# Gate tiles at the ends of attention's halves and ahead of retention's last transposes, another order of the first loads, and other ends of stages, in a three-layer fp32 network on one core

## The chip, the core and the metric

The kernel runs on one NeuronCore of a Trainium2 chip. Times are device microseconds (us) of one execution. The engines are TensorE (PE: matrix products, its weight loads shown as PEld), VectorE (DVE), ScalarE (ACT), GpSimd (POOL, nearly unused here) and SyncE (SP), which issues the transfers (DMAs). Each engine works through its own instructions in order; engines wait for each other by semaphores.

## The reference, cut to what matters

The input is 512 tokens of width 1024, all in fp32. Two hybrid layers come first. Each has three branches that are gated and summed, then a product with a residual:

```
h = rms_norm(x, norm_g);  z = h @ w_in         # width 14848, split by branch
y_conv = conv_module(c_glu, c_gate, ...) @ w_conv_out      # 31 taps, LayerNorm, silu
y_ret  = retention_branch(r_q, r_k, r_v, r_gate, ...) @ w_ret_out      # 4 heads, both directions
y_attn = window_attention_branch(a_q, a_k, a_v, a_gate, ...) @ w_attn_out   # 16 heads, 4 kv heads
g = sigmoid(g_logit + b_gate)                  # one gate for each branch and column
x = x + (g[0] * y_conv + g[1] * y_ret + g[2] * y_attn) @ w_out
```

A third layer of another kind follows: a gated MLP over blocks of tokens, a gated linear recurrence with 8 heads (HGRN2), a LayerNorm after each residual, a small gated embedding (256 wide) and a feed-forward part 2816 wide with a last LayerNorm.

## The kernel before, in words

Activations lie in the on-chip memory (SBUF) with features on the partitions, as 8 tiles of 128 x 512, except where tokens are wanted on the partitions. All products are fp32 by three matmuls: each operand is split into a high part, cast to fp32r, and the remainder; `mm3` (lines 172 to 174) issues high x high, high x low and low x high into one accumulator. So a tile of 128 x 512 over 1024 inputs is 8 x 3 = 24 matmuls of 512 columns.

The weights come as 509 chunks of 512 KB in the order in which they are used. `_load_raw` (L128) issues a chunk's DMA on SP's queue; `_split_next` has ACT cast it (`hi`, L147 or L149) and DVE subtract (`lo`, L150). There are three buffers of each kind (WB = 3), so hi and lo are made up to two chunks ahead. `take` hands out blocks and splits further as it goes. Chunks in HOLD are kept in ordinary slots until several passes have used them.

The program is written as Python generators: one yields after each tile of a product ("dense" work), the other after each step of an attention or retention or recurrence core. `weave` alternates a step of the one with steps of the other. A scheduler then places every instruction on its engine by its own estimate of times, with the order in which the code issued them as priority. `issue_after` puts an instruction behind a named other one.

The seams that the change touches:

- the start: SP's queue sends the gains (`vkt`), the 8 tiles of x (L1414), the first weight chunks, then the constants (`ckt`, L1419) whose first 128 columns are the identity matrix. ACT and DVE scale and split x tile by tile; DVE also sums the squares (L210), and PE adds those up over partitions (L244). The matrix `two`, twice the identity, is made by DVE as soon as the constants come (L217).
- attention: `att_core(l, g)` does one half of the heads in 8 pieces: scores (L812), softmax on ACT and DVE, transposes (L789), products with v (L768, L769). `conv_ab` gives the dense tiles beside it. After the first half the second half's q is projected (`att_q`), normed and rotated on DVE while gate tiles run (`att_gate`), then transposed (L673); after the second half `branch_out` multiplies by w_attn_out, each output tile behind its own merge-gate tile.
- retention: for each of 4 heads `ret_core` does scores and values; at its end ACT copies the result (L607), DVE takes mean and variance, ACT normalizes (L223), and PE transposes (L624). `ret_gate` and `ret_qk` are the dense work.
- norms over tokens (`norm_tokens`, `norm_tile`): each tile of 128 tokens is normed on DVE with a reciprocal root made of small integer and float operations on one column (`rsqrt`), and transposed back (L363).
- HGRN2: `hg_core` steps of two heads alternate (`weave_gen`), and `weave2` runs them beside dense tiles; the scores are products at L1092.
- the last stage (`down`): tokens 256 to 511 (tiles 2 and 3) do the last weights one tile after the other, from weights kept in SBUF, then norm and store.

## Time and profile before

| what | value |
|---|---|
| median of 3 runs | 3061.37 us (3060.49 to 3064.32) |
| profiled execution, own time | 3065.6 us |
| its span in the trace | 3063.8 us |
| granted TensorE clock, mean | 0.996 |
| PE busy | 3009.6 us (98%), 13932 matmuls |
| DVE busy | 2089.7 us (68%) |
| ACT busy | 1161.2 us (38%) |
| DMA | 288.97 MB, mean 94 GB/s |

The span runs from the first instruction to the last. Busy time counts an engine's instructions; what is left is idle time, and the trace says what each idle stretch ended with. The granted clock is the share of full speed that TensorE was given: 1.00 stands for 2.4 GHz, 0.50 for 1.2 GHz. A matmul of 512 columns takes 0.39 us in the trace at full clock and overlaps the next one, and 0.63 us at half clock.

### The profile page before, as it was taken

What the parts mean: (1) busy time and instruction counts of PE and PEld (TensorE: products, weight loads), DVE (VectorE), ACT (ScalarE), POOL (GpSimd) and SP (SyncE); (2) the same over time, 40 slices, a digit from 0 to 9 for tenths busy, and PEclk for the clock granted to TensorE, in tenths of its full rate; (3) what the DMA queues carried; (4) which work ended last, traced back from release to release, by engine and by line L of the source; (5) the groups of instructions that cost most, each with busy time, mean ns of one, the idle gap of its engine ahead of it and who ended that gap; (6) DMA issues with size and microseconds to landing.
All of it is one profiled execution on the core that took longest, in us unless ns stands there. A gap on an engine that the chain in (4) does not pass through costs nothing.

```text
span 3063.8 us, 36027 instructions
## 1 busy us (share of the span) xinstructions
PE 3009.6 (98%) x13932; PEld 2455.5 (80%) x13932; DVE 2089.7 (68%) x3791; ACT 1161.2 (38%) x1867; POOL 0.2 (0%) x4
## 2 busy tenths in 40 slices
PE   8999999999999999999999999999999999999998
PEld 6777888887888877778888788887888888788887
DVE  7778897877444677989787754467776654743326
ACT  5546223334233455632333433333543333422222
POOL 0000000000000000000000000000000000000000
PEclk9999999999999999999999999999999999999999
DMA  4121222221223322122222132254222223422234
GB/s 156 63 76 56 90 90 76 79 76 67 96 96 127 121 69 69 57 89 97 72 73 76 65 101 96 96 180 143 84 89 70 69 76 121 161 93 99 98 110 151
DMA packets 83979, 288.97 MB, mean 94 GB/s; under 512 B 9440, under 2 KB 9696, under 8 KB 83680
## 3 DMA queue, kind: packets, MB, share of 16 engines
q1 hardware_dynamic: 83808, 286.68, 27.8%
q8 instruction: 109, 1.79, 0.2%
q14 instruction: 62, 0.51, 0.1%
HBM read 282.45 MB, written 4.19 MB: 94 GB/s over the span
## 4 chain that ended last, share of the span: by engine, by line
PE 87%; DVE 8%; ACT 3%; issue 1%; DMA 1%; SPq 0%; DVEq 0%; ACTq 0%
PE pm L172 20%; PE pm L173 20%; PE pm L174 20%; PE pa L172 7%; PE pa L174 7%; PE pa L173 7%; ACT s L223 2%; DVE s L213 2%; DVE lo L150 1%; DVE s L210 1%; PE pi L789 1%; DVE s L206 1%; PE pa L1092 1%; DVE pa L814 1%; ACT hi L149 1%
## 5 line engine op out<-in xcount | busy, mean ns | idle before, releaser
L172 PE MATMUL pm<-s,hi 128*128 128x512 f32 x2848 | 1117.8, 393 | 4.0 <-ACT s L205 1.5
L173 PE MATMUL pm<-s,hi 128*128 128x512 f32 x2848 | 1115.9, 392 | 1.3 <-DVE s L206 1.3
L174 PE MATMUL pm<-s,lo 128*128 128x512 f32 x2848 | 1112.8, 391 | 0.5 <-DVE lo L150 0.5
L149 ACT CAST hi<-raw 128x1024 fp32r<-128x1024 f32 x497 | 523.0, 1052 | 1375.8 <-PE pm L173 735.1
L150 DVE TENSOR_TENSOR lo<-raw,hi 128x1024 fp32r<-128x1024 f32 x500 | 610.2, 1220 | 484.7 <-ACT hi L149 478.4
L172 PEld LDWEIGHTS pm<-s,hi 128*128 128x128 f32 x2848 | 534.8, 188 | 120.4 <-ACT s L205 3.5
L174 PEld LDWEIGHTS pm<-s,lo 128*128 128x128 f32 x2848 | 535.1, 188 | 112.3 <-issue 2.2
L173 PEld LDWEIGHTS pm<-s,hi 128*128 128x128 f32 x2848 | 535.2, 188 | 112.0 <-DVE s L206 3.5
L213 DVE SCALAR_TENSOR_TENSOR s<-s,m,s 128x497 f32<-128x497 f32 (+10 forms) x528 | 390.3, 742 | 11.4
L172 PE MATMUL pa<-hi,s 128*128 128x512 f32 x830 | 331.7, 400 | 8.8 <-ACT hi L147 6.6
L173 PE MATMUL pa<-lo,s 128*128 128x512 f32 x830 | 329.5, 397 | 3.1 <-DVE lo L150 3.1
L174 PE MATMUL pa<-hi,s 128*128 128x512 f32 x830 | 328.9, 397 | 0.0
L213 DVE SCALAR_TENSOR_TENSOR s<-s,pm 128x512 f32<-128x512 f32 x164 | 111.9, 682 | 140.8 <-PE pm L174 140.2
L172 PEld LDWEIGHTS pa<-hi,s 128*128 128x128 f32 x830 | 158.3, 191 | 42.7 <-ACT hi L147 6.6
L173 PEld LDWEIGHTS pa<-lo,s 128*128 128x128 f32 x830 | 158.4, 191 | 36.9 <-DVE lo L150 5.4
L174 PEld LDWEIGHTS pa<-hi,s 128*128 128x128 f32 x830 | 158.4, 191 | 32.4
L205 ACT CAST s<-s 128x512 fp32r<-128x512 f32 x184 | 110.8, 621 | 177.9 <-DVE s L213 137.9
L206 DVE TENSOR_TENSOR s<-s,s 128x512 fp32r<-128x512 f32 x184 | 123.4, 688 | 29.6 <-ACT s L205 28.2
L210 DVE TENSOR_TENSOR s<-s,s 128x512 f32<-128x512 f32 (+2 forms) x178 | 114.2, 662 | 1.7
L223 ACT ACTIVATE s<-s 128x512 f32<-128x512 f32 (+1 forms) x130 | 79.2, 627 | 89.3 <-DVE s L217 24.7
L213 DVE SCALAR_TENSOR_TENSOR s<-s,s 128x512 f32<-128x512 f32 (+2 forms) x194 | 103.7, 554 | 7.8 <-ACT s L223 6.2
L223 ACT ACTIVATE s<-pa,m 128x256 f32<-128x256 f32 (+2 forms) x136 | 69.2, 524 | 53.0 <-DVE m L213 50.0
(161 smaller groups left out, 2350.8 us busy)
## 6 DMA issues: line engine op xcount, KB each, us to landing
raw<-w SPq DMA_DIRECT2D x509, 512.0 KB, 3.3
s<-xT SPq DMA_DIRECT2D x16, 256.0 KB, 5.1
xd<-s SPq DMA_DIRECT2D x8, 256.0 KB, 2.0
s<-xd SPq DMA_DIRECT2D x8, 256.0 KB, 5.6
out<-s SPq DMA_DIRECT2D x8, 256.0 KB, 3.7
s<-c_ln_g SPq DMA_DIRECT2D x6, 256.0 KB, 4.7
s<-c_ln_b SPq DMA_DIRECT2D x6, 256.0 KB, 5.2
ckt<-ck SPq DMA_DIRECT2D x1, 1344.0 KB, 6.2
```

Of the source, the lines that this page charges most:

```text
L149: self.A.copy(h, raw)
L150: self.V.tensor_tensor(out=l, in0=raw, in1=h.bitcast(F32), op=ALU.subtract)
L172: T.matmul(out, lhsT=lh, rhs=rh, start=start, stop=False)
L173: T.matmul(out, lhsT=lh, rhs=rl, start=False, stop=False)
L174: T.matmul(out, lhsT=ll, rhs=rh, start=False, stop=stop)
L205: self.A.copy(h, src)
L206: self.V.tensor_tensor(out=l, in0=src, in1=h.bitcast(F32), op=ALU.subtract)
L210: return self.V.tensor_tensor(out=out, in0=a, in1=b, op=op)
L213: return self.V.scalar_tensor_tensor(out=out, in0=a, scalar=s, in1=b, op0=op0, op1=op1)
L223: return self.A.activation(out, a, f, bias=bias, scale=scale, **kw)
L789: t = T.transpose(ps[:, i * 128:i * 128 + 128], pr[i][:, x * 128:x * 128 + 128], self.ck("ident"))
L814: self.V.tensor_tensor_reduce(out=sps[i][:, 0:w], in0=sps[i][:, 0:w], in1=mask, scale=1.0, scalar=-3.0e38, op0=ALU.add, op1=ALU.max, accum ...
```

## The change

It has seven parts.

1. First loads: the first weight chunk, then the first x tile, then the gains, then the rest as before. The doubling that makes `two` is issued after the weight transfer that `load_rest` waits for, instead of after the first loads.
2. Attention: two gate tiles of the second half (`att_gate(l, 1, 0..1)`) are appended to the dense work of the first half's core; two merge-gate tiles (`branch_gate(l, 2, 0)` and `(l, 2, 1)`) to that of the second half's core. `branch_gate` is the first part of `branch_out`, taken out; finished gates wait in `self.gates`, and `branch_out` takes them from there.
3. Retention: the last head's work is written out by hand. Two merge-gate tiles of retention's branch and the first step of its output product stand ahead of the core's last transposes, and the parts of earlier heads are split one by one as they are asked for.
4. Norms: `ahead` splits the next weight chunks before a late step; the second step of tile 2's transposes goes behind the last product, into the generator that the caller takes on.
5. `rsqrt` of one column: -0.5 v is made once, and each of the three rounds is two operations instead of three.
6. HGRN2: the first step of both heads of a pair is issued ahead of the pair's dense work.
7. Last stage: KEEP_2 = 2 more chunks are held, so that tiles 2 and 3 each do their last ten weights (30 matmuls) alone instead of six (18).

```diff
+HOLD = set(range(C_OUT, C_OUT + KEEP_0)) | set(range(C_O, C_O + KEEP_1)) | set(range(NCHUNK - WB - KEEP_2, NCHUNK - WB))
...
+    def ahead(self):
+        while self.nsplit <= min(self.pos // 8 + WB - 1, NCHUNK - 1):
+            self._split_next()
...
+        if self.pos >= 64:
+            self.ahead()
         yield ps
...
+        if n == 1:
+            w = self.small([128, 1])
+            self.ts(w, v, -0.5, None, ALU.mult)
         for _ in range(3):
-            self.tt(a, y, y, ALU.mult)
-            self.stt(a, a, -0.5, v, ALU.mult, ALU.mult)
+            if n == 1:
+                self.ts(a, y, y, w, ALU.mult, ALU.mult)
...
-                                ((3,), self.acc, {0: 2, 1: 1, 2: 1, 6: 2, 7: 2})):
+                                ((3,), self.acc, {0: 2, 1: 1, 2: 1, 7: 2})):
...
                 if k in at:
+                    self.ahead()
                     next(late[at[k]])
...
-        return late[3]
+        def left():
+            next(late[2])
+            for _ in range(3):
+                next(late[3])
+                yield
+        self.ahead()
+        return left()
...
+    def branch_gate(self, l, i, m):
+        pg = self.fm(("w_in", l), O_GL + i * D + m * 128, self.h)
+        t = self.slot()
+        self.act(t, pg, AF.Tanh, scale=0.5, bias=self.hbg[:, i * 8 + m:i * 8 + m + 1])
+        self.gates.append(t)
+        yield
...
         for m in range(KT):
-            pg = self.fm(("w_in", l), O_GL + i * D + m * 128, self.h)
...
+            if not self.gates:
+                yield from self.branch_gate(l, i, m)
+            t = self.gates.pop(0)
...
+        with self.tc.issue_after(self.ready.ins):
+            self.ts(self.two, self.ck("ident"), 2.0, None, ALU.mult)
...
-        self.weave(self.conv_ab(l, range(0, 4)), self.att_core(l, 0))
+        self.weave(chain(self.conv_ab(l, range(0, 4)), self.att_gate(l, 1, range(0, 2))), self.att_core(l, 0))
...
-        self.weave(self.att_gate(l, 1), qpost, 1)
-        self.weave(self.conv_ab(l, range(4, 8)), self.att_core(l, 1))
+        self.weave(self.att_gate(l, 1, range(2, 4)), qpost, 1)
+        self.weave(chain(self.conv_ab(l, range(4, 8)), self.branch_gate(l, 2, 0), self.branch_gate(l, 2, 1)), self.att_core(l, 1))
...
+        out = self.branch_out(l, 1, ("w_ret_out", l), ys)
+        core = self.ret_core(3)
+        for i, _ in enumerate(self.ret_gate(l, 3)):
+            self.unit()
+            if i == 3:
+                ys[2]
+            next(core)
         self.bg_rate = RATES[3]
...
+        self.go(self.branch_gate(l, 1, 0))
+        next(core)
+        next(core)
+        self.go(self.branch_gate(l, 1, 1))
+        next(out)
+        self.unit()
+        for _ in core:
+            pass
+        self.go(out)
...
             c = self.weave_gen(self.hg_core(2 * p), self.hg_core(2 * p + 1))
+            next(c)
+            next(c)
             self.weave2(dense(p), c)
...
-        for tiles, pool, kept in (((0, 1), self.mm, 0), ((2, 3), self.acc, 2 * WB)):
+        for tiles, pool, kept in (((0, 1), self.mm, 0), ((2, 3), self.acc, 2 * (WB + KEEP_2))):
...
-        nc.sync.dma_start(self.vkt[:, o:o + w], self.ap["vk"][:, o:o + w])
         xs = [self.slot() for _ in range(KT)]
+        self._load_raw()
         for k in range(KT):
             nc.sync.dma_start(xs[k], self.ap["xT"][k])
-            if k in (0, 2, 5):
+            if k == 0:
+                nc.sync.dma_start(self.vkt[:, o:o + w], self.ap["vk"][:, o:o + w])
+            if k in (2, 5):
                 self._load_raw()
```

How instructions move, at three places. Line numbers are those of each program: `mm3` is L172 to L174 before and L180 to L182 after, a scaling `stt` L213 and L223, a `tt` L210 and L220, the lo of a chunk L150 and L153, the doubling L217 and L227. Buffer numbers follow the underscore.

DVE at the program's start, before (`two` is the doubled identity, `lo` a chunk's remainder, s_125 the sum of squares):

```order
L213 SCALAR_TENSOR_TENSOR s_122<-s_93,vkt,s_121 128x512
L150 TENSOR_TENSOR lo_208<-raw_102,hi_207 128x1024
L213 SCALAR_TENSOR_TENSOR s_128<-s_94,vkt,s_127 128x512
L217 TENSOR_SCALAR two<-ckt 128x128
L210 TENSOR_TENSOR s_125<-s_125,s_131 128x512
L213 SCALAR_TENSOR_TENSOR s_135<-s_95,vkt,s_134 128x512
L150 TENSOR_TENSOR lo_214<-raw_106,hi_213 128x1024
L210 TENSOR_TENSOR s_125<-s_125,s_138 128x512
```

and after (the sum is s_124):

```order
L223 SCALAR_TENSOR_TENSOR s_121<-s_92,vkt,s_120 128x512
L153 TENSOR_TENSOR lo_207<-raw_100,hi_206 128x1024
L223 SCALAR_TENSOR_TENSOR s_127<-s_93,vkt,s_126 128x512
L220 TENSOR_TENSOR s_124<-s_124,s_130 128x512
L223 SCALAR_TENSOR_TENSOR s_134<-s_94,vkt,s_133 128x512
L153 TENSOR_TENSOR lo_213<-raw_106,hi_212 128x1024
L220 TENSOR_TENSOR s_124<-s_124,s_137 128x512
```

The doubling has left this place; the steps of the sum follow each other without it.

PE at the end of attention's first half in layer 0, before (L789: transposes of the probabilities, L768 and L769: products with v, then q's projection into pa_1786):

```order
L789 MATMUL pi_1678<-ckt,s_1610 128x128
L789 MATMUL pi_1678<-ckt,s_1609 128x128
L789 MATMUL pi_1678<-ckt,s_1607 128x128
L789 MATMUL pi_1678<-ckt,s_1608 128x128
L768 MATMUL pi_1728<-s_1674,s_369 128x512
L769 MATMUL pi_1728<-s_1675,s_369 128x512
L768 MATMUL pi_1728<-s_1683,s_372 128x512
L769 MATMUL pi_1728<-s_1684,s_372 128x512
L172 MATMUL pa_1786<-hi_1508,s_341 128x512
```

and after (the same transposes are L818; pm_1728 is a gate tile of the second half):

```order
L180 MATMUL pm_1728<-s_340,hi_1508 128x512
L181 MATMUL pm_1728<-s_341,hi_1508 128x512
L182 MATMUL pm_1728<-s_340,lo_1509 128x512
L818 MATMUL pi_1678<-ckt,s_1610 128x128
L818 MATMUL pi_1678<-ckt,s_1609 128x128
L818 MATMUL pi_1678<-ckt,s_1607 128x128
L818 MATMUL pi_1678<-ckt,s_1608 128x128
L180 MATMUL pm_1728<-s_345,hi_1508 128x512
L181 MATMUL pm_1728<-s_346,hi_1508 128x512
L182 MATMUL pm_1728<-s_345,lo_1509 128x512
L180 MATMUL pm_1728<-s_351,hi_1508 128x512
L181 MATMUL pm_1728<-s_352,hi_1508 128x512
```

A gate tile stands around the transposes, 24 matmuls of which three are ahead of them.

DVE at the program's end, before (s_21243 and s_21244 are tile 2's halves, s_21422 and s_21423 tile 3's; L1335 and L1339 are the statistics):

```order
L210 TENSOR_TENSOR s_21423<-s_21423,pa_23955 128x512
L210 TENSOR_TENSOR m_24178<-m_24177 128x1
L1335 BN_STATS m_23411<-s_21423 128x6
L213 SCALAR_TENSOR_TENSOR m_24178<-m_24178,m_24173 128x1
L1339 BN_AGGR m_24216<-m_23411 128x2
L213 SCALAR_TENSOR_TENSOR m_24177<-m_24178,m_24177 128x1
L217 TENSOR_SCALAR m_24217<-m_24216 128x1
L213 SCALAR_TENSOR_TENSOR s_21422<-s_21422,m_24216,s_23400 128x512
L213 SCALAR_TENSOR_TENSOR s_21243<-s_21243,m_24177,s_23404 128x512
L213 SCALAR_TENSOR_TENSOR s_21244<-s_21244,m_24177,s_23405 128x512
L217 TENSOR_SCALAR m_24220<-m_24217 128x1
L213 SCALAR_TENSOR_TENSOR s_21423<-s_21423,m_24216,s_23401 128x512
```

and after (tile 3's halves are s_21415 and s_21416, the statistics L1381 and L1385):

```order
L223 SCALAR_TENSOR_TENSOR m_24163<-m_24164,m_24163 128x1
L223 SCALAR_TENSOR_TENSOR s_21243<-s_21243,m_24163,s_23396 128x512
L223 SCALAR_TENSOR_TENSOR s_21244<-s_21244,m_24163,s_23397 128x512
L220 TENSOR_TENSOR s_21416<-s_21416,pa_23947 128x512
L1381 BN_STATS m_23403<-s_21416 128x6
L1385 BN_AGGR m_24213<-m_23403 128x2
L227 TENSOR_SCALAR m_24214<-m_24213 128x1
L223 SCALAR_TENSOR_TENSOR s_21415<-s_21415,m_24213,s_23392 128x512
L227 TENSOR_SCALAR m_24217<-m_24214 128x1
```

Before, tile 2's last steps stand between those of tile 3; after, they are ahead of tile 3's add.

## Rows read from the trace of the kernel before

**Rows 1.** the page: busy time of each engine, share of the span, instructions
```profile
PE 3009.6 (98%) x13932; PEld 2455.5 (80%) x13932; DVE 2089.7 (68%) x3791; ACT 1161.2 (38%) x1867; POOL 0.2 (0%) x4
```

**Rows 2.** waits of PE, whole span: us in total, times, longest us
```profile
PE pi L789 <- ACT s L223: 6.4, 18, 0.6
PE pa L1092 <- DVE s L210: 3.2, 4, 0.9
PE pa L173 <- DVE lo L150: 3.1, 4, 1.3
PE pi L363 <- DVE s L213: 2.5, 3, 1.9
...
PE pa L172 <- ACT s L223: 2.1, 2, 1.1
PE pi L789 <- DVE s L206: 2.0, 2, 1.0
PE pi L624 <- ACT s L223: 1.9, 6, 0.4
...
PE pm L172 <- ACT s L205: 1.5, 2, 0.8
PE pi L624 <- DVE s L213: 1.3, 2, 0.7
PE pm L173 <- DVE s L206: 1.3, 6, 0.2
...
PE pi L769 <- DVE s L206: 1.1, 2, 0.5
```

**Rows 3.** busy time by stretch: length, each engine, PEclk, DMA share, GB/s
```profile
26.00:32.80 6.80, 6.80 (x21) 5.64 (x21) 4.04 (x17) 0.00 (x0) 0.00 (x0) 0.50 0.32 111
169.40:172.70 3.30, 3.30 (x10) 2.52 (x9) 2.20 (x8) 1.72 (x5) 0.00 (x0) 0.50 0.00 0
303.00:309.00 6.00, 4.47 (x15) 2.28 (x14) 4.09 (x9) 3.60 (x7) 0.00 (x0) 1.00 0.22 81
2074.10:2077.40 3.30, 3.30 (x9) 2.13 (x8) 1.34 (x6) 1.79 (x6) 0.00 (x0) 0.50 0.02 5
2681.60:2684.90 3.30, 3.30 (x9) 2.65 (x8) 1.22 (x2) 0.41 (x1) 0.00 (x0) 0.50 0.54 164
```

**Rows 4.** timeline of the start: start, us, instruction, [idle before, releaser]
```profile
4.08 0.72 ACT L223 ACTIVATE s<-s,vkt 128x512 fp32r<-128x512 f32 x1 [1.86 <-DMA s<-xT]
5.51 1.04 ACT L147 CAST hi<-raw 128x1024 fp32r<-128x1024 f32 x1 [0.70 <-DMA raw<-w]
...
13.93 0.23 DVE L217 TENSOR_SCALAR two<-ckt 128x128 f32<-128x128 f32 x1 [5.44 <-DMA ckt<-ck]
...
16.61 0.50 PE L173 MATMUL pa<-lo,s 128*128 128x512 f32 x1 [1.16 <-DVE lo L150]
...
25.81 1.74 PE L244 MATMUL pi<-ones,s 128*128 128x1 f32 x8 [2.33 <-DVE s L210]
```

**Rows 5.** timeline of PE and ACT at the end of retention, first layer
```profile
717.90 0.39 PE L173 MATMUL pa<-s,s 128*128 128x512 f32 x1
718.13 0.39 PE L174 MATMUL pa<-s,s 128*128 128x512 f32 x1
...
722.84 2.93 ACT L223 ACTIVATE s<-s,m,m 128x512 f32<-128x512 f32 x4 [3.64 <-DVE m L213]
```

**Rows 6.** timeline of PE ahead of the gated embedding
```profile
2679.98 0.50 PE L172 MATMUL pm<-s,hi 128*128 128x512 f32 x1 [1.18 <-ACT hi L149]
```

**Rows 7.** timeline of DVE, q of attention's second half, first layer
```profile
207.99 0.28 DVE L210 TENSOR_TENSOR s<-m,m 128x128 f32<-128x128 f32 x1
```

**Rows 8.** timeline of PE and DVE at the end of the program
```profile
3052.26 0.39 PE L174 MATMUL pa<-hi,s 128*128 128x512 f32 x1
...
3052.98 0.68 DVE L210 TENSOR_TENSOR s<-s,pa 128x512 f32<-128x512 f32 x1
...
3054.73 2.06 DVE L213 SCALAR_TENSOR_TENSOR s<-s,m,s 128x512 f32<-128x512 f32 x3
```

More of the change, by code (lines that the diff above doesn't have):

```diff
@@ L2 @@
 from contextlib import ExitStack
+from itertools import chain
 import numpy as np
@@ L64 @@
 C_O = C_OUT + 8 + 2 * (8 - KEEP_0) + 4 + 64 + 16
-HOLD = set(range(C_OUT, C_OUT + KEEP_0)) | set(range(C_O, C_O + KEEP_1))
+KEEP_2 = 2
+HOLD = set(range(C_OUT, C_OUT + KEEP_0)) | set(range(C_O, C_O + KEEP_1)) | set(range(NCHUNK - WB - KEEP_2, NCHUNK - WB))
 class Kern:
@@ L91, in __init__ @@
         self.first = {}
+        self.gates = []
         self.bg = None
@@ L231, in rsqrt @@
         self.ts(y.bitcast(I32), i, -1.0, float(0x5F3759DF), ALU.mult, ALU.add)
+        if n == 1:
+            w = self.small([128, 1])
+            self.ts(w, v, -0.5, None, ALU.mult)
         for _ in range(3):
-            self.tt(a, y, y, ALU.mult)
-            self.stt(a, a, -0.5, v, ALU.mult, ALU.mult)
+            if n == 1:
+                self.ts(a, y, y, w, ALU.mult, ALU.mult)
+            else:
+                self.tt(a, y, y, ALU.mult)
+                self.stt(a, a, -0.5, v, ALU.mult, ALU.mult)
             self.stt(y, a, 1.5, y, ALU.add, ALU.mult)
@@ L900, in layer, with parts @@
         self.go(self.ret_qk(l, 0), self.ret_v(l, 0))
-        for hd in range(4):
-            def dense(hd=hd):
-                yield from self.ret_gate(l, hd)
-                if hd < 3:
-                    yield from self.ret_qk(l, hd + 1)
-            core = self.ret_core(hd)
-            self.weave(dense(), core, 1)
-            if hd < 3:
-                self.go(self.ret_v(l, hd + 1))
-        self.bg_rate = RATES[3]
-        ys = Late([lambda y=y: self.split(y) for y in self.yr])
-        self.yr = None
-        self.go(self.branch_out(l, 1, ("w_ret_out", l), ys))
-        ys = None
+        for hd in range(3):
+            self.weave(chain(self.ret_gate(l, hd), self.ret_qk(l, hd + 1)), self.ret_core(hd), 1)
+            self.go(self.ret_v(l, hd + 1))
+        yr = self.yr
+        def parts(i):
+            y, yr[i] = yr[i], None
+            return self.split(y)
+        ys = Late([lambda i=i: parts(i) for i in range(16)])
+        out = self.branch_out(l, 1, ("w_ret_out", l), ys)
[5 more added lines that the diff above has]
+            next(core)
+        self.bg_rate = RATES[3]
+        self.go(self.branch_gate(l, 1, 0))
[7 more added lines that the diff above has]
+        self.go(out)
+        ys = out = core = yr = self.yr = None
         self.drain()
@@ L1425, in run @@
         self.two = self.cp.tile([128, 128], F32, name="two")
-        with self.tc.issue_after(self.dma.ins):
-            self.ts(self.two, self.ck("ident"), 2.0, None, ALU.mult)
         acc, xg = None, []
```

4 lines of the change are left out of this document (removed).

## The prediction

> **What bounds the kernel now.** I read the page first: TensorE (PE) is busy 3009.6 of 3063.8 us [rows 1], so all other engines together can win back only what PE doesn't work: 54.2 us of idle time, and the time in which PE works at half its clock. Nothing in the change removes a matmul; the built programs have 13,334 PE rows each. So the question is only which gaps close, which open, and where the clock falls.
>
> Next I read the list of waits of PE [rows 2]. It says who ends each gap: no wait is for a transfer once the first loads are in. Most of them are the ends of small chains on ACT and VectorE (DVE) at the seams between stages: PE has no tile of weights left to multiply, and the transposes or products of the stage's last piece are not ready. The largest group, 6.4 us at L789 in 18 pieces of at most 0.6, lies inside attention's halves; I leave it alone below, since the order there is the same.
>
> Last I read the granted clock [rows 3]. Some waits cost more than themselves. Behind them PE runs at 1.2 GHz instead of 2.4 (granted 0.50) for 3.4 us, in one case 6.8, and each such stretch costs half its length, 1.7 or 3.4 us. The stretch at 303 to 309 has 1.53 us of idle time in several pieces (6.00 less 4.47) and kept 1.00; the ones at 26, 169.4 and 2074.1 come behind idle time of 2.3, 2.6 and 1.9 us.
>
> **The change, part by part.** All against the profiled execution's 3065.6 us (span 3063.8 and 1.8 around it).
>
> *Start.* SP now sends the first weight chunk ahead of the first x tile and of the gains. In before the first scaling on ACT waits for x until 4.08, and the cast of chunk 0 waits for the chunk until 5.51, after which PE starts [rows 4]. ACT's order is unchanged (scaling, then cast), so an earlier chunk alone brings nothing, and x behind 512 KB more comes later: the scaling would start at some 5.1 and the cast at 5.8. I take +0.3, from -0.5 (chunk early, x hardly later) to +0.8.
> What brings more is DVE. It stood 5.44 us at the doubling of the identity matrix (tile two), waiting for that constant's transfer, with everything else queued behind it; then it worked through from 13.93 to the last sum of squares, which let PE go on at 25.81. PE had waited 1.16 us for lo of the second chunk and 2.33 us for that sum at L244 [rows 4], and then ran 6.8 us at half clock [rows 3]. The doubling now stands behind the sum. The same 11.8 us of work, begun 5.4 us earlier, ends at about 20.4; PE, without the first wait, gets to L244 at about 22. Both waits go: 1.16 + 2.33 + 3.4 - 0.3 = 6.6 us won. If x comes so late that PE still waits and the clock falls as before, it is 2; 7.4 at most.
>
> *End of attention's first half.* In each layer two gate tiles of the second half (24 matmuls each) are put among the last transposes and probability products, where PE now waits 1.0 (L789 for DVE), 0.54 (L769) and 1.05 (first projection of q, for ACT): 5.2 us in the two layers [rows 2]. Then the clock falls for 3.4 us in both layers (169.4 in the first [rows 3]), 1.7 us each. 48 matmuls at 0.23 us (two starts in a row of PE [rows 5]) give 10.9 us of cover for a chain that leaves 2.6 us open. I take 2.6 + 1.7 + 0.3 for slow restarts = 4.6 per layer, 9.2 in all; 4 if each wait halves and one clock fall stays; 10 at most.
> What pays: the second half's q has two gates behind it instead of four. By order, the first transposes of q come 62 matmuls (14.1 us) behind the projection instead of 96 (21.8). DVE, which also works on the convolution's taps there, is done with the first tile's rotation only at 208.3 [rows 7], and the transposes that read it may now wait about 1 us per layer. That is inside the range, not in the sum.
>
> *End of the second half.* Two merge-gate tiles (48 matmuls) stand ahead of the last products. The waits there are 1.5 us for casts on ACT and 1.3 for their remainders on DVE (L172 and L173 of pm) in two layers [rows 2], and some 0.4 of restarts per layer; the clock held. I take 3.6 won; from 1 to 4.6.
>
> *Retention.* Behind the last head's products the transposes at L624 waited 1.9 us for ACT and 1.3 for DVE in both layers [rows 2]. The last product starts at 718.13 and ACT's normalization of its result ends at 725.77, 7.6 us later; now 37 matmuls (8.4 us) stand between, two gate tiles among them, instead of 21. So the waits should go: 3.0 won. But DVE gets five splits earlier there, about 0.7 us each, and if all stand ahead of the normalization it is 3.5 us late and nothing is won; from 0 to 4.
>
> *Norms.* The reciprocal root of one column has 9 small operations instead of 11, next weights are split ahead of the late steps, and the second half of tile 2's transposes moves behind the last product. Waits touched: 1.94 of the 2.5 us at L363, with a clock fall behind it [rows 2, 3], and 1.34 of the 3.1 us for lo (L173). Two operations fewer at 0.2 us and one split out of the way don't close 1.94 us; the moved transposes do part of it. I take 2.0 won of 5.0, from 0 to 5. The wait before the gated embedding (1.18 us at 2680 [rows 6]) and its clock fall are in the same order as before: no change.
>
> *HGRN2.* The first DVE steps of both heads are put ahead of the dense tiles. PE waited four times at L1092, 3.2 us [rows 2]. I take 3.0, from 1 to 4.
>
> *End.* Behind the last matmul DVE finishes tile 2 between the steps of tile 3: its last add starts at 3052.98, 0.3 us behind the matmul's end, and two of the three scalings of the row at 3054.73 are tile 2's [rows 8]. With ten weights kept instead of six, tile 2 is done 30 matmuls (6.8 us) ahead of the end instead of 18 (4.1). By order nothing of it is left behind tile 3's add: that takes away 1.7 us (two scalings of 0.69 and three small operations of 0.12), 0.4 for two of tile 3's own small ones, and 0.3 at the start of the add. 2.3 won; from 1 to 2.6.
>
> **Sum.** 6.6 + 9.2 + 3.6 + 3.0 + 2.0 + 3.0 + 2.3 = 29.7 us. 3065.6 - 29.7 = 3035.9 for a profiled run. The median of the runs shown, 3061.37, lies 4.2 lower, so the forecast is 3031.7, say 3032. The bounds of the parts summed are 9 and 38 us; they will not all fall to one side, so its own range is 3022 to 3046.
>
> Half clock is the largest item: 3.4 + 3 x 1.7 = 8.5 us, of which the sum takes 6.8 (all but the one at 2074.1). The rows show it behind 1.2 us (2680) to 2.6 us of waiting, and not behind 1.5 us in pieces. The Trainium skill, "TensorE: Matmul & The Clock Gate", Part 1 (The HAM clock gate), says that the throttled state is the default and that activity releases it, and that the gate's own time base runs on freely, whatever the kernel does, so that the number of slow matmuls differs from run to run. By that rule a gap that is only shortened may still bring the slow clock at another place, which speaks against booking the gain in full: the sum would then be 29.7 - 6.8, or 22.9. The trace can't settle it, since it shows one execution.
>
> **Rivals.**
> *The clock falls stay* (shorter gaps still bring them, elsewhere). For it: the matmuls at the start are slow too, and a wait left at L244 or behind the new gates may be enough. Against: 303 to 309 kept its clock. Without the 6.8 us of clock the sum is 22.9: 3061.4 - 22.9 = 3038.5.
> *The waits move instead of going.* The tiles put ahead are taken from later stages, which have less in front of them (q's transposes after two gates, the last branch with two gates fewer), so that half comes back. For it: the rotation at 208 is that late because DVE has other work between its steps [rows 7]. Against: the later stages are long runs of independent tiles. 3061.4 - 14.9 = 3046.5.
> *Slower: late weight splits.* Tiles put ahead need their chunk's hi and lo earlier, and ACT and DVE work in order; a chunk stuck behind a core's steps stops all of PE's queue. The price of one is in the trace: at 2680 PE waited 1.18 us for a hi [rows 6] and soon ran at half clock for 3.4 us [rows 3], 2.9 us together. Some 30 chunks change place (gates, retention's splits, the norms). From ten such stalls on, the gain is gone; with fourteen, 41 - 30 = 11 us are lost: 3072. Against it: the three buffers of chunks, each good for 24 matmuls or more, are kept full in the new order at each place that I looked at.
> *It doesn't do what it says*: the new tiles wait themselves and the same chain still ends last: 3061.
>
> **How the numbers follow.** Forecast 0.66; clock falls stay 0.13; waits move 0.12; no effect 0.04; late splits 0.05. Faster and slower are counted from 0.2% (6.1 us), about what a measurement of this kernel can tell from no change: faster 0.66 + 0.13 + 0.12 less 0.01 for the weak end of the third, 0.90; same 0.05; slower 0.05. The range reaches from the forecast's low side, 3020, to the third case with room, 3050.
>
> **What would show it.** In the new profile L244 has no wait and PE's clock is 1.00 at 26 us; no pair of L789/L769 waits with a slow stretch behind it in either layer; no L1092 group; L624 below 1 us; the span ends about 8.8 us behind PE's last matmul instead of 11.2. PE's busy time falls by the half clock saved (some 7 us) and its idle time from 54 to about 31. It is wrong if new groups of waits for hi or lo, or at L702 (q's transposes), come to more than 8 us, or if slow stretches stand where none were.

## The result, and the profile after

The changed kernel takes 3040.26 us (median of 4 runs, 3037.96 to 3043.26), against 3060.96 for the kernel before (4 runs, 3060.49 to 3064.32). The ratio is 0.9929, with a 95% interval of 0.9917 to 0.9942: 0.7% faster, 20.7 us. The forecast was 3032, 29 us less, with a range that holds the time.

The profiled execution took 3038.11 us, its span is 3036.3. Against the profiled execution of before that is 27.5 us less, close to the sum that was forecast for it (29.7), but in part by luck: the one profile is of a long run and the other of a short one, and the medians differ by only 20.7. PE is busy 2996.7 us and idle 39.6 (54.2 before). One of six later executions of the changed kernel took 3691.94 us at a mean granted clock of 0.762; it is left out of all that follows.

The waits of PE after the change, over the whole span, as in [rows 2] (us in total, times, longest):

```profile
PE pi L818 <- ACT s L233: 6.8, 16, 0.6
...
PE pm L180 <- ACT s L233: 3.6, 3, 1.4
PE pi L387 <- DVE s L223: 2.5, 2, 1.9
...
PE pa L181 <- DVE lo L153: 1.6, 2, 1.3
PE pm L180 <- DVE s L223: 1.4, 2, 0.7
...
PE pm L180 <- ACT s L215: 0.7, 2, 0.3
...
PE pa L1136 <- DVE s L220: 0.3, 1, 0.3
```
Line numbers have moved: L789 is L818, L363 is L387, L1092 is L1136, and `mm3` is L180 to L182. The groups of [rows 2] that ended attention's halves are gone (L789 and L769 for DVE's remainders, the first projection for ACT, the casts and remainders of the second half), and so are those of retention's transposes. L1092's 3.2 us are 0.3. L363's are the same. And there is a new group near the top: 3.6 us in which a product (pm) waited for ACT at L233, three times. One of the three, 0.8 us ahead of HGRN2, was there before; two of 1.4 us are new. The 1.4 us for DVE at L223 are 0.7 in each layer's retention branch, new too, and so are the 0.7 us for casts on ACT (L215), 0.35 in each layer beside retention's last transposes.

The stretches with their length, each engine's busy time and PEclk, as in [rows 3]:

```profile
26.00:32.80 6.80, 6.80 (x29) 5.26 (x29) 5.23 (x8) 2.92 (x4) 0.00 (x0) 1.00 0.48 176
155.00:162.00 7.00, 6.88 (x36) 5.37 (x33) 4.91 (x19) 3.39 (x13) 0.00 (x0) 1.00 0.25 75
217.00:222.00 5.00, 3.60 (x18) 2.57 (x18) 4.83 (x13) 3.47 (x9) 0.00 (x0) 1.00 0.10 16
2050.00:2058.00 8.00, 5.71 (x25) 3.30 (x23) 7.43 (x18) 4.44 (x11) 0.00 (x0) 1.00 0.24 77
```
The first two answer to the rows at 26 and 169.4: no half clock, and PE works through. In the third PE is idle 1.4 us of 5. The fourth is the seam to the third layer: 2.3 us idle, 1.94 of them the wait at the norm's transposes that before had too [rows 2], but the clock stayed at 1.00 this time.

The start, ACT and DVE, as in [rows 4]:

```profile
5.04 0.72 ACT L233 ACTIVATE s<-s,vkt 128x512 fp32r<-128x512 f32 x1 [2.82 <-DMA vkt<-vk]
...
19.68 0.69 DVE L220 TENSOR_TENSOR s<-s,s 128x512 f32<-128x512 f32 x1
20.28 0.22 DVE L227 TENSOR_SCALAR two<-ckt 128x128 f32<-128x128 f32 x1
```
The first scaling now waits for the gains and starts at 5.04 (4.08 before), the cast of the chunk follows it at once, and the last sum of squares is started at 19.68, with the doubling behind it at 20.28. PE started at 6.75 instead of 6.61 and didn't wait for the sum.

The new wait, in the first layer, behind the second half's q: DVE's last rotation, then ACT, then PE:

```profile
212.46 0.29 DVE L220 TENSOR_TENSOR s<-m,m 128x128 f32<-128x128 f32 x1
...
216.98 0.59 ACT L215 CAST s<-pi 128x512 fp32r<-128x512 f32 x1 [0.31 <-PE pi L702]
217.96 1.05 ACT L152 CAST hi<-raw 128x1024 fp32r<-128x1024 f32 x1 [0.39 <-PE pm L181]
218.91 0.59 ACT L233 ACTIVATE s<-pm 128x512 f32<-128x512 f32 x1
...
219.56 0.50 PE L180 MATMUL pm<-s,hi 128*128 128x512 f32 x1 [1.40 <-ACT s L233]
```
ACT stands in order: the last of the casts of q's transposes at 216.98, behind transposes that PE could do only after DVE's last rotation (212.46), then the cast of a weight chunk, whose buffer PE had just freed, and only then, at 218.91, the tanh that reads a gate's product. PE needs that product's buffer for its next tile and waits 1.40 us until 219.56.

The end, PE's last matmul and DVE's steps of tile 3, as in [rows 8]:

```profile
3026.57 0.39 PE L182 MATMUL pa<-hi,s 128*128 128x512 f32 x1
...
3027.00 0.69 DVE L220 TENSOR_TENSOR s<-s,pa 128x512 f32<-128x512 f32 x1 [0.49 <-PE pa L182]
...
3031.90 1.41 DVE L223 SCALAR_TENSOR_TENSOR s<-s,m,s 128x512 f32<-128x512 f32 x2
```
Nothing of tile 2 stands between the add (3027.00) and the two last scalings (3031.90). From PE's last matmul to the end of the span it is 9.4 us, 11.1 before.

### The profile page after: what moved, and what is told of

Its sections match the earlier page's. It is cut to its first block, busy times and chain, and to the rows that moved or that the text cites. A ratio compares the mean times of both kernels' runs of the same rounds, so it can differ in the third digit from the quotient of the medians.

```text
span 3036.3 us, 35977 instructions
## 1 busy us (share of the span) xinstructions
PE 2996.7 (99%) x13932; PEld 2449.3 (81%) x13932; DVE 2084.6 (69%) x3769; ACT 1159.6 (38%) x1869; POOL 0.2 (0%) x4
## 4 chain that ended last, share of the span: by engine, by line
PE 89%; DVE 7%; ACT 3%; issue 1%; DMA 0%; SPq 0%; DVEq 0%; ACTq 0%
PE pm L180 20%; PE pm L182 20%; PE pm L181 20%; PE pa L181 7%; PE pa L180 7%; PE pa L182 7%; ACT s L233 2%; DVE s L223 2%; DVE lo L153 1%; DVE s L220 1%; PE pi L818 1%; ACT hi L152 1%; DVE s L216 1%; PE pa L1136 1%; PE pa L841 1%
## 5 line engine op out<-in xcount | busy, mean ns | idle before, releaser
L180 PE MATMUL pm<-s,hi 128*128 128x512 f32 x2848 | 1120.1, 394 | 7.1 <-ACT s L233 3.6
L182 PE MATMUL pm<-s,lo 128*128 128x512 f32 x2848 | 1112.1, 391 | 0.5 <-DVE lo L153 0.5
L153 DVE TENSOR_TENSOR lo<-raw,hi 128x1024 fp32r<-128x1024 f32 x498 | 608.4, 1222 | 509.1 <-ACT hi L152 503.1
L180 PEld LDWEIGHTS pm<-s,hi 128*128 128x128 f32 x2848 | 534.8, 188 | 125.2 <-issue 5.6
L182 PEld LDWEIGHTS pm<-s,lo 128*128 128x128 f32 x2848 | 534.8, 188 | 111.7 <-issue 1.2
L223 DVE SCALAR_TENSOR_TENSOR s<-s,m,s 128x497 f32<-128x497 f32 (+10 forms) x528 | 390.7, 743 | 10.8
L180 PE MATMUL pa<-hi,s 128*128 128x512 f32 x822 | 324.6, 396 | 7.0 <-ACT hi L150 6.7
L181 PE MATMUL pa<-lo,s 128*128 128x512 f32 x822 | 322.9, 393 | 1.7 <-DVE lo L153 1.6
L182 PE MATMUL pa<-hi,s 128*128 128x512 f32 x822 | 322.1, 392 | 0.0
L223 DVE SCALAR_TENSOR_TENSOR s<-s,pm 128x512 f32<-128x512 f32 x164 | 112.1, 683 | 161.6 <-PE pm L182 161.2
L180 PEld LDWEIGHTS pa<-hi,s 128*128 128x128 f32 x822 | 154.8, 188 | 39.1 <-ACT hi L150 6.7
L215 ACT CAST s<-s 128x512 fp32r<-128x512 f32 x184 | 110.7, 620 | 188.0 <-DVE s L223 145.7
L182 PEld LDWEIGHTS pa<-hi,s 128*128 128x128 f32 x822 | 154.8, 188 | 32.2 <-DVE s L220 0.4
L220 DVE TENSOR_TENSOR s<-s,s 128x512 f32<-128x512 f32 (+2 forms) x178 | 114.6, 664 | 2.3
L233 ACT ACTIVATE s<-s 128x512 f32<-128x512 f32 (+1 forms) x130 | 78.4, 627 | 81.6 <-DVE s L227 24.7
L223 DVE SCALAR_TENSOR_TENSOR s<-s,s 128x512 f32<-128x512 f32 (+2 forms) x194 | 103.8, 555 | 7.9 <-ACT s L233 6.0
L233 ACT ACTIVATE s<-pa,m 128x256 f32<-128x256 f32 (+2 forms) x136 | 69.3, 527 | 38.6 <-DVE m L223 35.9
```

The costliest lines, as they stand in the source:

```text
L153: self.V.tensor_tensor(out=l, in0=raw, in1=h.bitcast(F32), op=ALU.subtract)
L180: T.matmul(out, lhsT=lh, rhs=rh, start=start, stop=False)
L181: T.matmul(out, lhsT=lh, rhs=rl, start=False, stop=False)
L182: T.matmul(out, lhsT=ll, rhs=rh, start=False, stop=stop)
L215: self.A.copy(h, src)
L220: return self.V.tensor_tensor(out=out, in0=a, in1=b, op=op)
```

## Experiments

Positions say where time is lost. P1 is the start of attention's first scores in layer 0, P2 the same in layer 1, P3 the first transposes of the norm ahead of the third layer, all read from PE's timeline in us; "slow" lists where PE's products begin to run at half clock for 1.5 us or more, behind the program's first 15 us.

| kernel | P1 | P2 | P3 | PE's end | span | slow |
|---|---|---|---|---|---|---|
| before | 94.72 | 1108.71 | 2040.07 | 3052.65 | 3063.8 | 26, 169, 1183, 2074, 2682 |
| before_again | 93.11 | 1107.02 | 2038.46 | 3049.83 | 3061.0 | 27, 167, 1181, 2073 |
| changed | 86.86 | 1094.86 | 2020.15 | 3026.96 | 3036.3 | none |
| after_again | 88.21 | 1097.66 | 2022.91 | 3030.44 | 3039.8 | 222 |
| old_loads | 88.09 | 1097.55 | 2022.79 | 3029.44 | 3038.8 | 221 |
| no_att_gates | 87.17 | 1099.21 | 2027.19 | 3033.59 | 3042.9 | 162 |
| no_ret | 88.21 | 1100.35 | 2030.87 | 3040.19 | 3049.5 | 718, 1731, 2065, 2669 |
| no_hg | 86.85 | 1094.67 | 2019.93 | 3031.78 | 3041.1 | 2660 |
| no_keep | 87.29 | 1096.67 | 2021.87 | 3028.85 | 3039.6 | 221, 2056 |
| no_norms | 87.83 | 1097.25 | 2022.46 | 3029.06 | 3038.4 | 221 |
| taps_pt | 87.37 | 1090.73 | 2011.55 | 3018.86 | 3028.2 | none |
| one_gate_pt | 87.00 | 1091.61 | 2013.67 | 3020.65 | 3030.0 | none |
| taps_psplit | 87.34 | 1090.99 | 2011.89 | 3019.24 | 3028.6 | 2046 |
| taps_pmid | 87.99 | 1091.49 | 2012.36 | 3017.22 | 3026.6 | none |

**before_again and after_again: both kernels unchanged.** The first question was why the medians differ less than the profiles.

> The kernel before, unchanged, to see several executions with their granted clock. Theory A (the falls of TensorE's clock differ from execution to execution): the runs spread over some 4 us, from about 3060.5 to 3065.5, and the longer ones have the lower mean clock, about 0.001 of clock for 1.5 us; a profile of a short run shows fewer stretches at half clock than the five of the first profile. Rival B (the falls are tied to the gaps and the same in each execution): all runs have the clock 0.996, and what spreads is something else; the profile shows the same stretches.

> The changed kernel, unchanged. Theory A: times in two groups, about 3038 at a clock of 0.999 and about 3042.5 at 0.997 to 0.998, and the median of a fresh set falls into either; the ratio to the kernel before stays between 0.992 and 0.994. If the profile is of a long run, it shows one or two stretches at half clock more than the first one did, behind waits that the short run has too. Rival B: the long runs have longer waits instead, and the same clock stretches.

The kernel before: median 3062.76 (11 runs, 3059.82 to 3065.62), at granted clocks of 0.995 (the longest) to 0.998. The changed kernel: 3038.46 to 3041.59 (median 3040.99) in five runs at 0.998 to 0.999. The new profiles show which it is. In before_again the stretch at 2681 is missing, with the same wait ahead of it as in [rows 6]; here that wait, and then two stretches behind waits that the first profile has as well, one at half clock (1180.9) and one that kept its clock (2679; PEclk is the third number from the right):

```profile
2678.78 0.50 PE L172 MATMUL pm<-s,hi 128*128 128x512 f32 x1 [1.18 <-ACT hi L149]
```
```profile
1180.90:1183.90 3.00, 3.00 (x9) 2.32 (x8) 1.60 (x6) 2.48 (x9) 0.00 (x0) 0.50 0.00 0
2679.00:2682.00 3.00, 2.47 (x11) 1.70 (x11) 2.27 (x3) 1.81 (x4) 0.00 (x0) 1.00 0.32 97
```
In after_again PE lost its clock behind the new wait, where the first profile kept it; first after_again, then the changed kernel, the same 3 us:

```profile
221.50:224.50 3.00, 3.00 (x9) 2.38 (x8) 1.85 (x5) 2.02 (x9) 0.00 (x0) 0.52 0.48 168
```
```profile
221.50:224.50 3.00, 3.00 (x20) 1.98 (x19) 2.00 (x9) 1.17 (x7) 0.00 (x0) 1.00 0.56 175
```
The lists of waits agree to 0.2 us in nearly all groups within each pair. So theory A holds: the falls differ from execution to execution behind the same waits. It holds less neatly than expected: there are no two groups of times for the changed kernel but a spread, and of the 3.5 us between its two profiles 1.35 arise before P1, at the start (last section). Compared at a run near each median (3061.0 and 3039.8 spans) the change is worth 21.2 us. An estimate, with half of each slow stretch taken off, which is the most that it can cost: before has 20.5 us of half clock and before_again 13.7, the changed kernel 0 and after_again 3.4, so the first pair of profiles differs by 27.5 - 10.2 = 17.3 us without the clock and the second by 21.2 - 5.1 = 16.1.

**old_loads: the first loads in the order of before.**

```diff
-        self._load_raw()
         for k in range(KT):
             nc.sync.dma_start(xs[k], self.ap["xT"][k])
-            if k == 0:
-                nc.sync.dma_start(self.vkt[:, o:o + w], self.ap["vk"][:, o:o + w])
-            if k in (2, 5):
+            if k in (0, 2, 5):
                 self._load_raw()
```

> The changed kernel with the first loads in the order of before; the doubling of the identity stays behind the sum of squares. Theory (the doubling is what held DVE): PE starts at 6.6 us, the two waits of the start stay away, no half clock at 26 us, span within 1 us of the changed kernel's at the same clock (3036.3 at 0.999). Rival (the order of the loads is needed too): a wait at the sum of squares or for the second chunk comes back, 1 to 2.5 us, and perhaps the half clock of 6.8 us with it.

P1 is 88.09, within 0.12 us of after_again, and no wait came back. (The changed kernel's own P1 is 1.2 us earlier, because its first products left half clock at 10.8 us; here it was 13.0, in after_again 13.4.) ACT, and PE's start:

```profile
5.95 1.04 ACT L150 CAST hi<-raw 128x1024 fp32r<-128x1024 f32 x1 [0.51 <-DMA raw<-w]
...
7.04 1.22 PE L180 MATMUL pa<-hi,s 128*128 128x512 f32 x2 [7.04 <-ACT hi L150]
```
PE starts at 7.04 in this order and at 6.75 and 6.98 in two executions of the new order. So the loads' order is worth nothing that can be told. Up to P1 this kernel differs from the one before only in the doubling, so the start's gain is the doubling that no longer blocks DVE.

**no_att_gates: the gates at the ends of attention's halves moved back.**

```diff
-chain(self.conv_ab(l, range(0, 4)), self.att_gate(l, 1, range(0, 2)))
+self.conv_ab(l, range(0, 4))
...
-self.weave(self.att_gate(l, 1, range(2, 4)), qpost, 1)
-chain(self.conv_ab(l, range(4, 8)), self.branch_gate(l, 2, 0), self.branch_gate(l, 2, 1))
+self.weave(self.att_gate(l, 1), qpost, 1)
+self.conv_ab(l, range(4, 8))
```

> The changed kernel without gate tiles at the ends of attention's halves (the four gates of the second half and the merge gates stand where they stood before). Theory: the waits behind both halves come back, 2.6 + 1.5 us in each layer and some restarts, and the new waits of 1.4 us for a product's buffer behind the second half's q go, so the span is 6 to 8 us longer than the changed kernel's at the same number of slow stretches, and 3.4 more where the clock falls behind both first halves. Rival (the waits only moved): within 3 us of the changed kernel.

From P1 to P3 it took 1940.0 us, 5.3 more than after_again (1934.7), with one slow stretch in both (1933.3 in the changed kernel's first profile, without one). The waits of before are back within 0.1 us, and the new ones of 1.4 us are gone; four of the groups:

```profile
PE pa L180 <- ACT s L233: 2.1, 2, 1.1
PE pi L818 <- DVE s L216: 2.1, 2, 1.0
...
PE pm L180 <- ACT s L215: 1.5, 2, 0.7
...
PE pm L180 <- ACT s L233: 0.8, 1, 0.8
```
The expectation's lower end was 6, so both theories miss by a little: if the gates close the 9.4 us of waits and restarts that the forecast counts without the clock, they open 4.1 of others, 2.8 of them the waits behind q.

**no_ret: the last head of retention as before.** The loop over four heads of the kernel before, and `branch_out` behind it.

```diff
-        for hd in range(3):
-            self.weave(chain(self.ret_gate(l, hd), self.ret_qk(l, hd + 1)), self.ret_core(hd), 1)
...
+        for hd in range(4):
...
+            self.weave(dense(), core, 1)
```

> The changed kernel with the last head of retention as before (no gate tiles ahead of the last transposes, parts split as before). Theory, from the two traces put side by side by their attention and norm anchors: the retention part is worth about 2 us in each layer, so PE's end comes some 3.9 us later than in the changed kernel at the same number of slow stretches, and the waits at the last transposes of retention (ACT 1.9, DVE 1.3) are back. Rival (new waits behind it, at a product's buffer and at the last scores, eat it): within 1 us.

From P1 to P3 it is 9.4 us longer (1942.7 against 1933.3 in the changed kernel), slow stretches included. The waits at the last transposes:

```profile
PE pi L653 <- ACT s L233: 3.3, 8, 0.9
...
PE pi L653 <- DVE s L223: 1.2, 2, 0.7
```
They are 4.5 us, not the 3.2 of [rows 2]. As much stands ahead of them as before (22 matmuls between the last product and the transposes, 21 before), but ACT's normalization starts 5.4 us behind that product instead of 4.7: DVE has an add of 128x512 (0.66 us at 708.50) among the steps of mean and variance that wasn't there. And the clock fell behind both, which it hadn't in either profile of before:

```profile
716.60:720.00 3.40, 3.40 (x11) 2.90 (x11) 3.40 (x5) 3.40 (x8) 0.00 (x0) 0.51 0.36 122
1727.00:1733.80 6.80, 6.13 (x19) 4.96 (x20) 6.18 (x10) 6.80 (x14) 0.00 (x0) 0.50 0.22 77
```
By the starts of PE's products and transposes in them against the same ones at full clock, an estimate, the two stretches cost some 1.6 and 2.4 us. So the part itself is worth about 5 us here, a little more than the 3.9 expected.

**no_hg, no_norms, no_keep: one part each undone.**

```diff
-            next(c)
-            next(c)
             self.weave2(dense(p), c)
```

> The changed kernel with HGRN2's first core steps behind the dense tiles again. Theory: the four waits of 0.6 to 0.9 us at the scores come back, PE's end 2.7 us later at the same number of slow stretches. Rival (their time is only moved to the next scores): within 1 us.

The four waits are back:

```profile
PE pa L1136 <- DVE s L220: 3.2, 4, 0.9
```
PE's end is 4.8 us later than the changed kernel's. The slow stretch at 2660 is 1.7 of it, and a wait for a lo near the end, which after_again has too, 0.5: 2.6 to 3.1 us are left, as expected.

```diff
-                    self.ahead()
                     next(late[at[k]])
...
-        return left()
+        return late[3]
```

> The changed kernel with the token norms' late steps and early splits as before (the shorter reciprocal root stays). Theory, from the waits that both first traces show there (1.9 us at the transposes, 1.3 for a lo, in both): the part is worth next to nothing, PE's end within 1 us at the same number of slow stretches. Rival (what the prediction booked): 2 us later.

From P3 to PE's end: 1006.6 us, 1006.8 in the changed kernel. The waits at the norms are the same in number and size as in the first fence of this document's result:

```profile
PE pi L379 <- DVE s L223: 2.4, 2, 1.9
...
PE pa L181 <- DVE lo L153: 1.6, 2, 1.3
```
So the late steps and the early splits ahead of them are worth nothing. The shorter reciprocal root stayed in; the longest of these waits is 1.94 us here, in the changed kernel and in the one before, so the root didn't shorten it either.

```diff
-KEEP_2 = 2
+KEEP_2 = 0
```

> The changed kernel with KEEP_2 = 0, so tile 2 is done 18 matmuls ahead of the end as before. Theory: PE's end where it was (within 0.5 us), the time behind PE's last matmul 1.4 us longer (10.7 instead of 9.4), since the interleaving of the two tiles on DVE is back and only the shorter reciprocal root is kept. Rival (the output transfer sets the end): the time behind PE stays 9.4.

PE's end to the span's end is 10.75 us, 1.4 more than with ten kept weights. PE's end itself is 1.9 us later than the changed kernel's; 1.7 of that arise ahead of P3 (the start and the stretch at 221), and from P3 on it is 0.2. PE's last matmul and a row of DVE:

```profile
3028.46 0.39 PE L182 MATMUL pa<-hi,s 128*128 128x512 f32 x1
...
3030.70 1.36 DVE L223 SCALAR_TENSOR_TENSOR s<-s,m,s 128x512 f32<-128x512 f32 x2
```
By the order of the steps the two scalings at 3030.70 are tile 2's: 1.9 us behind the end of PE's last matmul, with tile 3's still to come.

**taps_pt, one_gate_pt: two ways to take the new wait away.** In the first the convolution's taps start later, in the second q keeps three gates behind it. Both issue the loads of the embedding's tokens (`pT`) ahead of the gate products.

```diff
-        self.bg, self.bg_rate = self.conv_taps(l), RATES[0]
         self.weave(self.att_gate(l, 1, range(2, 4)), qpost, 1)
+        self.bg, self.bg_rate = self.conv_taps(l), RATES[0]
...
-        self.between(gates(), steps)
         pt = [self.slot(), self.slot()]
         for i in range(2):
             self.nc.sync.dma_start(pt[i], self.ap["pT"][i])
+        self.between(gates(), steps)
```

> The changed kernel with two edits at separate places: the convolution's taps start only after the two gates behind the second half's q, and the small embedding's tokens are loaded ahead of the gate products, not after them. Theory: DVE's taps make q's rotation late, ACT then stands at q's casts and reads the gate's product late, and so PE waits 1.4 us for a product's buffer in each layer with a fall of the clock behind it in most executions; without the taps there both go, 3 to 5 us. The loads remove the wait of 1.2 and 0.5 us behind the embedding's gates, 2 us. Together 5 to 7 us under the changed kernel, median 3034. Rival (the taps are only late elsewhere): the first half of the gain comes back at the product buffers of the branches (0.7 us each now), and the median stays above 3037.5.

> The changed kernel with one gate tile instead of two at the end of attention's first half (three stay behind the second half's q), and the embedding's tokens loaded early as in the other kernel. Theory: 24 matmuls (5.4 us) cover most of the 2.6 us of waits at the end of the half, and with three gates the wait of 1.4 us behind q goes too, so 2 to 4 us of gain there and 2 us at the embedding, median 3035 to 3037. Rival (the cover is used up to the last matmul): up to 2 us of the waits at the end of the half are back in each layer, with the clock falling behind them, and the median stays above 3038.

taps_pt: 3030.06 us (4 runs within 0.4 us), ratio to before 0.9894 (0.9878 to 0.9911). one_gate_pt: 3032.25 (3031.69 to 3034.71), 0.9903 (0.9888 to 0.9918). Both beat their expectation, and for one half of it the reason given was wrong. DVE's last rotation and ACT behind q in taps_pt, then PE and ACT at the embedding:

```profile
208.25 0.29 DVE L220 TENSOR_TENSOR s<-m,m 128x128 f32<-128x128 f32 x1
...
211.93 0.59 ACT L215 CAST s<-pi 128x512 fp32r<-128x512 f32 x1 [0.32 <-PE pi L702]
212.41 0.61 ACT L233 ACTIVATE s<-pm 128x512 f32<-128x512 f32 x1
...
2646.69 0.50 PE L180 MATMUL pm<-s,hi 128*128 128x512 f32 x1 [1.18 <-ACT hi L152]
...
2645.59 1.04 ACT L152 CAST hi<-raw 128x1024 fp32r<-128x1024 f32 x1
2646.54 1.15 ACT L233 ACTIVATE s<-s 128x512 f32<-128x512 f32 x2
2647.60 1.12 ACT L215 CAST s<-s 128x512 fp32r<-128x512 f32 x2
```
Without the taps between them the rotations are done 4.2 us earlier (208.25, 212.46 in the changed kernel). Behind q the last cast now comes at 211.93 and the tanh right behind it at 212.41, early enough: PE has no wait there in either layer, and the layers are 4.6 and 4.5 us shorter (P1 to P2 1003.4 against 1008.0 us, P2 to P3 920.8 against 925.3). The rival's place, the product's buffer in retention's branch, lost its wait too. In layer 0 the waits that went are 1.40, 0.72 and 0.35 us; the rest of the 4.6 stands in no list of waits, and where it comes from stays open. The four runs lie within 0.4 us, which fits a wait that brought the clock down in some executions only; but one_gate_pt, without that wait too, spreads over 3 us, so it isn't shown. The waits of 1.18 and 0.52 us at the embedding are unchanged. The tokens had landed long before; their casts (2647.60) stand on ACT behind the weight cast (2645.59) and two tanh.

**taps_psplit, taps_pmid: the token splits earlier as well.** In the first the line moves ahead of the gate products:

```diff
+        p = [self.split(x) for x in pt]
         self.between(gates(), steps)
-        p = [self.split(x) for x in pt]
```

> The kernel with the later taps and the early loads, and now the splits of the embedding's tokens also stand ahead of the gate products. Theory: in the run before, the tokens were there early but their casts stood on ACT behind the cast of the next weight chunk, so PE took a tile of the feed-forward part first, whose chunk had no free buffer before the last gate product; with the splits early PE goes on with the embedding's product, whose chunk is ready, and the waits of 1.18 and 0.52 us go, 1.9 us of PE's end: span 3026.3 and median 3028.2. Rival (the splits disturb the norm steps that are on DVE and ACT at that time): the wait for a lo there, 1.3 us, grows by as much and the median stays at 3030.

The rival was right in the time, 3029.48 us, no more than 0.6 under taps_pt, but not in the wait that it named: the one for a lo didn't grow. The waits of 1.18 and 0.52 are gone, and those at the norm's transposes rose from 2.4 to 3.8 us, since ACT's cast of the tokens at 2602.70 waited 1.59 us for their transfer with the norm's casts (L393) behind it:

```profile
PE pi L387 <- DVE s L223: 3.4, 2, 1.9
...
PE pi L387 <- DVE s L220: 0.4, 1, 0.4
...
2602.70 0.62 ACT L215 CAST s<-s 128x512 fp32r<-128x512 f32 x1 [1.59 <-DMA s<-pT]
2603.22 0.26 ACT L393 CAST s<-pi 128x128 fp32r<-128x128 f32 x1
```
In the second they stand at the start of the second gate product:

```diff
             for g in range(2):
+                if g == 1:
+                    p.extend(self.split(x) for x in pt)
                 for ps in self.tm("w_ple_gate_2", g * 512, h1, g == 0):
```

> As the kernel before it, but the splits of the embedding's tokens stand at the start of the second gate product, behind the last norm step. Theory (the splits hurt only because they ran into the norm's steps): the waits of 1.18 and 0.52 us stay away and those at the norm's transposes are back at 2.4 us in all, so PE's end is 1.9 us earlier than in the kernel that only loads early, median 3028.2. Rival (the second gate product needs ACT and DVE for its weights as well): a wait for a hi or lo of 1 us or more appears there and the median stays between 3029.5 and 3030.

3028.16 us (3027.86 to 3028.38), ratio to before 0.9890 (0.9874 to 0.9907). What is left of PE's larger waits:

```profile
PE pi L818 <- ACT s L233: 7.2, 20, 0.6
...
PE pi L387 <- DVE s L223: 2.5, 2, 1.9
PE pa L181 <- DVE lo L153: 2.2, 3, 1.3
```
This version beats both kernels: 33 us under the one before, 12 to 13 under the changed one.

## Why the prediction was right, step by step

The direction, the order of size and the range were right. That the first profile lay 27.5 us lower, near the 29.7 of the sum, was luck in part. Without the clock the sum is 22.9 us, and the pairs of profiles give 16 to 17; the first pair made it up with 10.2 us of half clock where the sum had 6.8. The steps, with their terms:

| part | forecast | measured | from |
|---|---|---|---|
| start | 6.6, 3.4 of it clock | 7.9 and 4.9, clock in it | P1 in the two pairs |
| attention's ends | 12.8, 3.4 of it clock | 5.3, without the clock | no_att_gates, equal clock |
| retention | 3.0 | about 5 | no_ret, less its slow stretches |
| norms | 2.0 | 0 | no_norms |
| HGRN2 | 3.0 | 2.6 to 3.1 | no_hg, less its slow stretch |
| end | 2.3 | 1.8 | PE's end to span |

*Start.* The mechanism was right and shown by old_loads: DVE's queue was blocked by the doubling. That an earlier chunk would bring nothing was right too. 3.5 us of it are the two waits; the rest is the clock, and that differs between executions. The stretch at 26 lasted 6.8 us in one profile of before and 3.4 in the other, and the first products leave half clock 10.8 to 13.4 us into the program in these four. So the term has a spread of 3 us that the prediction gave only to a rival.

*Attention.* This is the term that was mis-sized. The waits that it counted did go, all of them. What failed is the sentence that the price of two gates fewer behind q "is inside the range, not in the sum", at about 1 us per layer at q's transposes. They waited 0.3 us in both layers together. The price appeared one step on, in a way that was not thought of: ACT, in order, stood behind the late transposes' casts with a gate's product unread, and PE lacked its buffer, 1.4 us per layer in the wait alone; taps_pt shows that the taps there cost about 4.5 us per layer, with the wait in retention's branch. DVE's taps between q's rotations were the cause, together with the two gates fewer (one_gate_pt, which gives one back, has no such wait either), as the rival of moved waits had it. That rival's forecast (3046.5) was too gloomy, and the main one too bright.

*The clock.* The sum booked 6.8 us for falls that go. Its total of 8.5 us left out the stretch at 2681.6, which stands in [rows 3]; with it half clock costs 10.2. All the waits behind which the booked ones fell went, and at the start and behind the first halves no fall was seen again in the profiles of kernels with the change in place. But a new wait of 1.4 us brought a fall of its own at 221 in four of the seven profiles that have it; a slow stretch where none was is one of the prediction's own signs of being wrong. And the falls at 2074 and 2682 are missing in the changed kernel's first profile though their waits (1.94 and 1.18 us) stayed, where the prediction had no change. So the rival "the clock falls stay, elsewhere" (3038.5) is nearest to the median. The Trainium skill says of the gate's time base ("TensorE: Matmul & The Clock Gate", Part 1) that it runs on freely. The two profiles of before agree with that: the wait of 1.18 us has a fall behind it in the first and none in before_again.

*From the profile to the median.* The forecast subtracted 29.7 us, worked out in one execution, from a median that was 4.2 us lower, without asking what the 4.2 were. before_again, a run at its median, is 2.8 us shorter than the first profile and has 6.8 us less of half clock, at the start and behind 2680. So some 3 us were half clock of the one execution and were booked twice; and the median of three runs was itself 1.1 us low (3062.5 in seventeen later ones).

*Retention* was under-sized, by its own bounds (0 to 4): the feared cost, five splits ahead of the normalization, didn't come, and undoing the part costs more than the waits seen in before, since these waits are longer with the other parts in place (4.5 us in no_ret, 3.2 before). *Norms*: two operations fewer ahead of a wait of 1.9 us changed nothing that can be measured; the forecast's lower bound. *HGRN2* and the *end* were right within 0.5 us. At the end the booked 0.4 us for two small operations was too much: a round of the root takes 0.50 us instead of 0.58 there, since the new double operation takes 0.27 where the simple one took 0.16.

What was said would show it: no wait at the sum of squares and 1.00 at 26 us (seen); no slow stretch behind the first halves (seen); no L1092 group (0.3 us left); L624 below 1 us (none left); 8.8 us behind PE's last matmul (9.4); idle time down to 31 us (39.6); busy time down by some 7 us (12.9). The 13,334 PE rows of the prediction stand in no trace; both have 13932 matmuls.

## What to carry to other kernels

Work put ahead to fill one gap is taken from a later place: ask there what the engine's queue holds behind the late step, since the wait may appear at a buffer that another engine has not read yet, and not at the step itself. Before a list of gains is taken from a median, sort the runs by granted clock and subtract the clock's share from the profiled one. A chain that other work interrupts on an in-order engine (here the taps between q's rotations) can be cheaper to clear than to cover.

## What the runs showed of the hardware

A fall of TensorE's clock is not tied to its gap. The wait of 1.4 us behind q stands in seven profiles, in both layers: in layer 0 a half-clock stretch followed in four of them, in layer 1 in none. The wait of 1.9 us at the norm's first transposes stands in all fourteen, with a half-clock stretch behind it in five. The wait of 1.18 us at the embedding stands in twelve, with one behind it in three.

A fall doesn't always cost half its length. In no_keep the stretch of 3.4 us at 2056 set PE back by only 0.6 us: at full clock PE waits there for a hi and a lo, 0.24 and 0.29 us in the changed kernel.

The first matmuls of the program run at half clock, though a row over the first 12 us reads 1.00; for the changed kernel, the row and two products:

```profile
0.00:12.00 12.00, 5.21 (x14) 3.73 (x15) 6.14 (x9) 8.45 (x13) 0.20 (x4) 1.00 0.87 309
```
```profile
10.31 0.63 PE L181 MATMUL pa<-lo,s 128*128 128x512 f32 x1
...
11.25 0.39 PE L181 MATMUL pa<-lo,s 128*128 128x512 f32 x1
```
The trace's record of the granted clock begins only at 10.8 us here, and the row counts what has no record as full clock. Up to that moment products take 0.63 us and start 0.43 us apart, the figures of half clock; from it on they take 0.39 and start 0.23 apart. In all fourteen profiles the spacing changes where the record begins, between 10.8 and 13.5 us, with 4 to 11 starts of 0.43 us ahead of it. That moves all that follows by up to 1.3 us from one execution to the next (P1 of the changed kernel: 86.86 and 88.21). What ends it can't be told from these traces.
